# A modulation row made earlier and two gate products ahead of a loop, in a transformer block on one core

## The chip, the core and the metric

The kernel runs on one core of a Trainium2 chip. The metric is the device time of one execution in microseconds (us), median of three runs. Engines: PE is TensorE (matmuls; PEld its weight loads), DVE VectorE, ACT ScalarE, POOL GpSimd, SP the engine that here issues most DMAs.

## The reference, cut to what matters

Two blocks run one after the other on 512 rows of width 1024. The change lies in the first.

```
mod = (cond @ w_ada[l] + b_ada[l]).reshape(b, 6, d)
shift1, scale1, gate1, shift2, scale2, gate2 = [mod[:, i] for i in range(6)]
hn = modulate(rmsnorm(x, norm1_g[l]), shift1, scale1)
proj = hn @ w_in[l]
qa, ka, va, qi, ki, wi, qb, kb, vb, ga, gb = jnp.split(proj, offsets, axis=-1)
ya = dsa_attention(qa, ka, va, qi, ki, wi, rel_bias)      # top-k mask from an index score of qi, ki, wi
yb = stick_breaking_attention(qb, kb, vb)
merged = jax.nn.sigmoid(ga) * (ya @ w_proj_a[l]) + jax.nn.sigmoid(gb) * (yb @ w_proj_b[l])
x = x + gate1[:, None, :] * (merged @ w_out[l])
...
```

`cond` is one vector of 1024 numbers, so each of the six modulation rows is a vector times a 1024 x 1024 piece of `w_ada`. The row of this change is `gate1`, which is first used after `w_out`.

## The kernel before

Everything is laid out with the model's width on the partitions. A matmul of full precision is three fp32r matmuls (lines 189 to 191, high x high, low x high, high x low): weights come by a 512 KB DMA into `raw`, ACT makes the high part `whi` (L183), DVE the low part `wlo` (L184), and 24 matmuls of 128x512 then give 128 output columns for all 512 rows. Such a run of 24 is called a product here. Products, PV sums and the modulation sum go through two PSUM banks `g`, scores and other sums through six banks `a`.

Block 1 goes through these stages (times in the span): norm and first products to 74 us; the **index stage** to about 125 us; **sb**, stick-breaking attention over 8 heads, to 255 us; **DA**, the masked attention over 8 heads, to 372 us; the **w_proj loop** over eight chunks n to 467 us; w_out after it.

In the index stage `vproj` (v of sb) is followed by 24 index units: two matmuls of kih/kil with qi, an ACT relu (L553) and a DVE sum into `iacc` (L555, L557). Then come `z0` and `z1`, the first scores of the sb heads 0 and 1 (L421, L422, L650), and two products for head pair 1 (called q1 and k1 here; they are the first two fills). The bias rows `rs` are made there too (L540 on PE, L541 on DVE).

`heads` runs the heads of sb and DA. Before each half head it calls fills by the table `B1F`: k is a product for a later head's q or k, g a gate product, t a step of the top-k search, v the second vproj, a half of a modulation row (`ada`), r its end (the `row` that `ada` returns). `WPF` is such a table for the w_proj loop.

`ada` loads eight 128x512 pieces of `w_ada`, two to a DMA of 512 KB, into `adaraw` (two buffers), and DVE sums them weighted with `cond` into the accumulator (L305 the first, L307 the other seven: one chain). `row` sums over the partitions on PE with a matrix of ones (L311), adds the bias on DVE (L314; with a gain also L318) and writes 512 numbers to `modrow` in HBM (L319). In DA all chains use one accumulator, `iacc` of the index stage.

Each engine works through its instructions in a fixed order, which a scheduler sets at build time from the program. An engine that waits holds back everything behind it. SP issues the DMAs in order in the same way.

At a DA head's end ACT copies half of the PV sum into `ya` (L455) and DVE adds the other half (L460); only then is that `g` bank free.

Of the kernel before, what the change touches and what calls it, by code (L numbers as in the profile page):

```python
# [11 lines left out]
F32 = mybir.dt.float32  # L12
# [5 lines left out]
AF = mybir.ActivationFunctionType  # L18
# [7 lines left out]
KC = 8  # L26
TB = 4
# [34 lines left out]
WX = 5  # L62
ADV = (5, 5, 5, 6, 7, 8, 8, 8)
B1F = ('kk', 'gt', 'kt', 'kt', 'gt', 't', 'kt', 'kt', 'gt', 't', 'kt', 'kt', 'gt', 'gt', 't', 'v',
       'ka', 'k', 'r', 'gk', 'a', 'k', 'r', 'gk', 'a', 'k', 'r', 'g', 'a', '', 'r', '')
WPF = ('', '', 'a', '', 'ra', 'ra', 'ra', 'r')
ADKB = 3
TG = 4
# [7 lines left out]
class Kern:  # L76
# [214 lines left out]
                nc.tensor.transpose(p[:, ts(t, 128)], src[:, t, ts(k, 128)], self.ident)  # L291
            self.hilo(hi[:, k], lo[:, k], p, None if scale is None else scale[:, k:k + 1])

    def ada(self, pool, acc, cond, col, dst_row, half, gain=None):
        nc, I = self.nc, self.I
        wv = I["w_ada"].rearrange("(k p) n -> p k n", p=128)
        c0 = col * D + half * 512
        for kc in range(0, KC, 2):
            raw = pool.tile([128, 2, 512], F32, tag="adaraw", bufs=2, name=self.nm("adaraw"))
            with self.tc.issue_after(self.loaded):  # L300
                nc.sync.dma_start(raw, wv[:, kc:kc + 2, c0:c0 + 512])
            for j in range(2):
                k = kc + j
                if k == 0:
                    nc.vector.tensor_scalar(acc, raw[:, 0], cond[:, 0:1], None, op0=ALU.mult)  # L305
                else:
                    nc.vector.scalar_tensor_tensor(acc, raw[:, j], cond[:, k:k + 1], acc, op0=ALU.mult, op1=ALU.add)  # L307

        def row():
            p = self.psg()  # L310
            nc.tensor.matmul(p, lhsT=self.onesf, rhs=acc, start=True, stop=True)  # L311
            bro = pool.tile([1, 512], F32, tag="adab", bufs=1, name=self.nm("adab"))
            nc.sync.dma_start(bro, I["b_ada"][0:1, c0:c0 + 512])
            nc.vector.tensor_tensor(acc[0:1], p[0:1], bro, op=ALU.add)  # L314
            if gain is not None:
                bro = pool.tile([1, 512], F32, tag="adab", bufs=1, name=self.nm("adab"))
                nc.sync.dma_start(bro, I[gain][0:1, half * 512:half * 512 + 512])
                nc.vector.scalar_tensor_tensor(acc[0:1], acc[0:1], 1.0, bro, op0=ALU.add, op1=ALU.mult)  # L318
            nc.sync.dma_start(self.modrow[dst_row:dst_row + 1, half * 512:half * 512 + 512], acc[0:1])  # L319
        return row  # L320
# [147 lines left out]
    def block1(self):  # L468
        nc, tc, I = self.nc, self.tc, self.I
        wv = I["w_in"].rearrange("(k p) n -> p k n", p=128)  # L470
        ctx = ExitStack()
        b1 = ctx.enter_context(tc.tile_pool(name="b1", bufs=1))
        hnh, hnl = self.act_pair()
# [12 lines left out]
        def vproj(c0, pool):  # L486
            v = pool.tile([128, TB, 8, 2, 64], F32R, tag="v", name=self.nm("v"))
            for half in range(2):
                outs = [self.psg(), self.psg()]
                for kc in range(0, KC, 4):  # L490
                    hi, lo = self.split_chunk(wv[:, kc:kc + 4, c0 + 256 * half:c0 + 256 * half + 256])
                    for j in range(4):
                        k = kc + j
                        for t in range(TB):
                            self.mm3(outs[t // 2][:, ts(t % 2, 256)], hnh[:, k, ts(t, 128)], hnl[:, k, ts(t, 128)],
                                     hi[:, j], lo[:, j], k == 0 and t % 2 == 0, k == KC - 1, skip=True)
                for i in range(2):
                    self.v_split(v, 2 * i, half, outs[i])
            return v

        with tc.tile_pool(name="p0", bufs=1) as p0:
            cond = self.load_cond(p0)
# [6 lines left out]
        with tc.tile_pool(name="pidx", bufs=1) as pi:  # L509
            pva = pat_ctx.enter_context(tc.tile_pool(name="pva", bufs=1, side="right"))  # L510
            rb = pva.tile([32, 8], F32, name="rb")
            oh = pva.tile([32, 640], F32, name="oh")
            rs = pva.tile([8, 640], F32, name="rs")
            nc.sync.dma_start(rb, I["rel_bias"])
            nc.sync.dma_start(oh, I["bucket"])
            rdr = self.dp.tile([8, 640], F32, name="rdr")
            r128 = self.dp.tile([8, 128, 640], F32, name="r128")
            p = outs[0]
            kih = pi.tile([128, 512], F32R, name="kih")
            kil = pi.tile([128, 512], F32R, name="kil")  # L520
            for q in range(2):
                nc.scalar.activation(kih[64 * q:64 * q + 64], p[0:64], AF.Copy)
            for q in range(2):
                nc.vector.tensor_tensor(kil[64 * q:64 * q + 64], p[0:64], kih[0:64], op=ALU.subtract)
            qi = [self.stack_out(pi, "qi", outs[1], bufs=4)]
            wiT = pi.tile([128, 512], F32, name="wiT")
            nc.scalar.activation(wiT[64:72], p[64:72], AF.Copy, scale=IDX_SCALE)
            pw = self.psg()
            wi = pi.tile([128, TB, 8], F32, name="wi")
            for t in range(TB):  # L530
                nc.tensor.transpose(pw[:, ts(t, 8)], wiT[64:72, ts(t, 128)], self.ident[64:72, 64:72])
            nc.vector.tensor_copy(wi.rearrange("p t h -> p (t h)"), pw[:, 0:32])
            vb = vproj(3144, pvb)
            qi += [self.stack_out(pi, "qi", outs[i], bufs=4) for i in range(2, 5)]
            qk["qb", 0] = self.dup_out(pat, "dup", outs[5], 0.125)
            qk["kb", 0] = self.stack_out(pat, "stk", outs[6])
            acc = {b: b1.tile([128, 128 * (b + 1)], F32, name=f"iacc{b}") for b in range(1, 4)}
            for j, (a0, n) in enumerate(((0, 512), (512, 128))):
                p = self.psg()
                nc.tensor.matmul(p[:8, :n], lhsT=rb, rhs=oh[:, a0:a0 + n], start=True, stop=True)  # L540
                nc.vector.tensor_scalar(rs[:, a0:a0 + n], p[:8, :n], -1.0, None, op0=ALU.mult)  # L541
            nc.sync.dma_start(rdr, rs)
            for h in range(H):
                nc.sync.dma_start(r128[h], rdr[h:h + 1].broadcast_to([128, 640]))
            for pr in range(4):
                for e in range(2):
                    h = 2 * pr + e
                    for b in (3, 2, 1):
                        nk = 128 * (b + 1)
                        s = self.psa()  # L550
                        self.mm2(s[:, :nk], qi[pr][:, e, ts(b, 128)], kih[:, :nk], kil[:, :nk], True, True)
                        rl = pi.tile([128, 512], F32, tag="relu", bufs=3, name=self.nm("relu"))
                        nc.scalar.activation(rl[:, :nk], s[:, :nk], AF.Relu)  # L553
                        if h == 0:
                            nc.vector.tensor_scalar(acc[b], rl[:, :nk], wi[:, b, 0:1], None, op0=ALU.mult)  # L555
                        else:
                            nc.vector.scalar_tensor_tensor(acc[b], rl[:, :nk], wi[:, b, h:h + 1], acc[b],  # L557
                                                           op0=ALU.mult, op1=ALU.add)
# [13 lines left out]
        gates = {}  # L572
# [134 lines left out]
            return pt  # L707

        pad = ctx.enter_context(tc.tile_pool(name="pad", bufs=1))
        adas = [(c, r, hf, g) for c, r, g in ((2, 0, None), (4, 1, "norm2_g"), (3, 2, None), (5, 3, None)) for hf in range(2)]  # L710
        rows = []
        fill["a"] = lambda: rows.append(self.ada(pad, acc[3], cond, *adas.pop(0)))
        fill["r"] = lambda: rows.pop(0)()
# [3 lines left out]
            heads(16, lambda h: da_s(pa, h), lambda st: self.transpose_p(pa, st, 2), va["v"], ya)  # L717
        pat_ctx.close()
        pm = ctx.enter_context(tc.tile_pool(name="pm", bufs=1))
        mh = pm.tile([128, KC, 512], F32R, name="mh")  # L720
        ml = pm.tile([128, KC, 512], F32R, name="ml")
        ys_ctx = ExitStack()
# [22 lines left out]
            for c in WPF[n]:  # L745
                fill[c]()
        xv = I["x"].rearrange("(t p) d -> p t d", p=128)
        for t in range((len(gates) + 1) // 2):
            nc.sync.dma_start(self.x[:, t], xv[:, t])
        ys_ctx.close()  # L750
        prm = ctx.enter_context(tc.tile_pool(name="prm", bufs=1))
# [865 lines left out]
```

## Time and profile before

| what | value |
|---|---|
| median of 3 runs | 2385.33 us (2384.72 to 2385.57) |
| profiled execution | 2384.28 us, its span 2382.4 us |
| PE / DVE / ACT busy | 97% / 73% / 43% of the span |
| chain that ended last | PE 91%, DVE 5% |
| DA stage, 273 to 372 us | PE busy 82.58 of 99 us, mean granted clock 0.90 |

The span is what the trace covers; the profiled execution took 1.9 us more around it. The median of the runs is 1.05 us above the profiled execution. The granted clock is a share of TensorE's full clock: 1.00 is 2.4 GHz, 0.50 is 1.2 GHz.

### The profile page before, as it was taken

The numbers are of one execution on the slowest core, as the hardware profiler recorded it, in microseconds if no ns is written. First come the engines' busy times: TensorE is split into PE (matmuls) and PEld (weight loads), VectorE is DVE, ScalarE is ACT, GpSimd is POOL, SyncE is SP. The second block draws the span as 40 slices with busy tenths as digits, with TensorE's granted clock in tenths as the row PEclk, the third lists the DMA queues.
The fourth block names the chain that finished last, engine by engine and source line by source line (L and its number), as shares of the span: only waits on it lengthen the run. The fifth ranks groups of instructions, "written<-read, shape, count | busy, mean of one in ns | idle before, by whom it ended". The sixth has DMA issues, their size and how long they took to land.

```text
span 2382.4 us, 33726 instructions
## 1 busy us (share of the span) xinstructions
PE 2302.8 (97%) x12405; PEld 2013.1 (85%) x12409; DVE 1744.0 (73%) x3421; ACT 1030.3 (43%) x1642; POOL 326.3 (14%) x286
## 2 busy tenths in 40 slices
PE   7999888999999999999999999999989989999999
PEld 6888766778899999999999988888868878888887
DVE  7689876677998998876888898888886765333321
ACT  3587444243355665553333333333345543322211
POOL 0000000000000323432344432222200000000000
PEclk9999999999999999999999999999989989999999
DMA  9432644652255999989999999999943312333231
GB/s 268 116 98 63 187 141 132 207 165 80 87 179 165 349 357 352 340 337 331 313 334 340 339 376 358 334 338 348 343 136 91 102 36 80 107 97 97 90 116 43
DMA packets 282217, 498.63 MB, mean 209 GB/s; under 512 B 19442, under 2 KB 176754, under 8 KB 280516
## 3 DMA queue, kind: packets, MB, share of 16 engines
q1 hardware_dynamic: 243268, 355.96, 44.8%
q0 software_dynamic: 38784, 140.53, 16.9%
q8 instruction: 97, 1.59, 0.3%
q14 instruction: 68, 0.56, 0.1%
HBM read 444.98 MB, written 47.76 MB: 207 GB/s over the span
## 4 chain that ended last, share of the span: by engine, by line
PE 91%; DVE 5%; ACT 1%; issue 1%; DMA 1%; SPq 0%; DVEq 0%; ACTq 0%
PE a L190 17%; PE a L189 17%; PE a L191 17%; PE g L189 11%; PE g L190 11%; PE g L191 10%; PE g L962 2%; PE a L421 1%; DVE wlo L184 1%; PE g L421 1%; PE g L422 1%; PE a L675 0%; PE a L422 0%; PE a L674 0%; DVE nl L257 0%
## 5 line engine op out<-in xcount | busy, mean ns | idle before, releaser
L183 ACT ACTIVATE whi<-raw 128x1024 fp32r<-128x1024 f32 x425 | 446.5, 1054 | 682.6 <-PE g L190 343.8
L184 DVE TENSOR_TENSOR wlo<-raw,whi 128x1024 fp32r<-128x1024 f32 x425 | 518.2, 1221 | 297.9 <-ACT whi L183 288.1
L189 PE MATMUL g<-nh,whi 128*128 128x512 f32 (+4 forms) x1024 | 384.2, 375 | 10.8 <-DVE ya L460 7.8
L190 PE MATMUL g<-nl,whi 128*128 128x512 f32 (+4 forms) x1024 | 383.3, 374 | 0.0
L191 PE MATMUL g<-nh,wlo 128*128 128x512 f32 (+4 forms) x1024 | 381.4, 372 | 0.0
L190 PE MATMUL a<-nl,whi 128*128 128x384 f32 (+2 forms) x912 | 309.8, 340 | 1.3 <-DVE nl L257 1.2
L189 PE MATMUL a<-nh,whi 128*128 128x384 f32 (+2 forms) x912 | 303.7, 340 | 3.4 <-ACT nh L256 3.3
L191 PE MATMUL a<-nh,wlo 128*128 128x384 f32 (+2 forms) x912 | 305.2, 335 | 0.4 <-DVE wlo L184 0.4
L190 PE MATMUL a<-wlo,ch 128*128 128x512 f32 x768 | 298.6, 389 | 0.0
L191 PE MATMUL a<-whi,cl 128*128 128x512 f32 x768 | 297.9, 389 | 0.0
L189 PE MATMUL a<-whi,ch 128*128 128x512 f32 x768 | 264.0, 389 | 0.0
L1038 POOL DMA_INDIRECT grow<-in_u_dram,eidx x128 | 152.4, 1191 | 764.2 <-DVE o_g L941 433.1
L189 PEld LDWEIGHTS g<-nh,whi 128*128 128x128 f32 (+1 forms) x1024 | 193.0, 188 | 42.3 <-DVE ya L460 8.4
L191 PEld LDWEIGHTS g<-nh,wlo 128*128 128x128 f32 (+1 forms) x1024 | 193.3, 189 | 29.5 <-issue 0.2
L190 PEld LDWEIGHTS g<-nl,whi 128*128 128x128 f32 (+1 forms) x1024 | 193.0, 188 | 29.5
L256 ACT ACTIVATE ch<-cf 128x384 fp32r<-128x384 f32 x128 | 67.1, 525 | 319.3 <-issue 182.9
L1038 POOL DMA_INDIRECT grow<-in_v_dram,eidx x128 | 159.4, 1246 | 318.4 <-DVE gacc L1056 269.7
L189 PEld LDWEIGHTS a<-nh,whi 128*128 128x128 f32 x912 | 173.6, 191 | 6.4 <-ACT nh L256 4.1
L190 PEld LDWEIGHTS a<-nl,whi 128*128 128x128 f32 x912 | 173.4, 190 | 4.6 <-DVE nl L257 2.0
L191 PEld LDWEIGHTS a<-nh,wlo 128*128 128x128 f32 x912 | 174.1, 191 | 2.9 <-DVE wlo L184 0.8
L191 PEld LDWEIGHTS a<-whi,cl 128*128 128x128 f32 x768 | 144.2, 188 | 29.8
L190 PEld LDWEIGHTS a<-wlo,ch 128*128 128x128 f32 x768 | 144.1, 188 | 28.9
(398 smaller groups left out, 3947.6 us busy)
## 6 DMA issues: line engine op xcount, KB each, us to landing
raw<-in_u_t_dram SPq DMA_DIRECT2D x128, 512.0 KB
raw<-in_v_dram SPq DMA_DIRECT2D x128, 512.0 KB
raw<-in_w_in_dram SPq DMA_DIRECT2D x54, 512.0 KB
gdr<-gblk SPq DMA_DIRECT2D x12, 2048.0 KB
vg<-gdr SPq DMA_DIRECT2D x192, 128.0 KB
udr<-ug SPq DMA_DIRECT2D x44, 384.0 KB
vu<-udr SPq DMA_DIRECT2D x44, 384.0 KB
adaraw<-in_w_ada_dram SPq DMA_DIRECT2D x32, 512.0 KB
```

What stands on the lines that cost most here:

```text
L183: nc.scalar.activation(hi, raw, AF.Copy)
L184: self.lastlo = nc.vector.tensor_tensor(lo, raw, hi, op=ALU.subtract).ins
L189: mm(out, lhsT=lh, rhs=rh, start=start, stop=False, skip_group_check=skip)
L190: mm(out, lhsT=lh, rhs=rl, start=False, stop=False, skip_group_check=skip)
L191: mm(out, lhsT=ll, rhs=rh, start=False, stop=stop, skip_group_check=skip)
L256: nc.scalar.activation(hi, src, AF.Copy)
L421: mm(out, lhsT=st, rhs=mh, start=start, stop=False, skip_group_check=skip)
L422: mm(out, lhsT=st, rhs=ml, start=False, stop=stop, skip_group_check=skip)
L962: nc.tensor.matmul(p[:, ts(j, 128)], lhsT=s2[:, c], rhs=rep[k][:, c // 2, :, c % 2], start=(i == 0), stop=(i == 1))
L1038: nc.gpsimd.indirect_dma_start(out=u, out_offset=None, in_=I[src], in_offset=bass.IndirectOffsetOnAxis(ap=eidx[:, i:i + 1], axis=0))
```

## The change

The first modulation row (column 2 of `w_ada`, `gate1`, both halves) leaves the fills of DA. It is made in the index stage right after `vproj`, with its own accumulators `adasum`, and with DMAs of one 128x512 piece (256 KB, eight per half instead of four). The second half of `B1F` is dealt anew: DA keeps the two halves of column 4. `WPF` is as it was. The gate products of chunk n=4 are written ahead of the w_proj loop, and ACT copies them to `gearly`; the loop then finds them in `gates`.

```diff
 B1F = (...
-       'ka', 'k', 'r', 'gk', 'a', 'k', 'r', 'gk', 'a', 'k', 'r', 'g', 'a', '', 'r', '')
+       'k', 'k', '', 'gk', 'a', 'k', '', 'gk', 'r', 'k', 'a', 'g', '', '', 'r', '')
...
-    def ada(self, pool, acc, cond, col, dst_row, half, gain=None):
+    def ada(self, pool, acc, cond, col, dst_row, half, gain=None, ks=2):
...
-        for kc in range(0, KC, 2):
-            raw = pool.tile([128, 2, 512], F32, tag="adaraw", bufs=2, name=self.nm("adaraw"))
+        for kc in range(0, KC, ks):
+            raw = pool.tile([128, ks, 512], F32, tag="adaraw", bufs=2, name=self.nm("adaraw"))
...
             vb = vproj(3144, pvb)
+            for half in range(2):
+                asum = pi.tile([128, 512], F32, tag="adasum", name=self.nm("adasum"))
+                self.ada(pi, asum, cond, 2, 0, half, ks=1)()
...
-        adas = [(c, r, hf, g) for c, r, g in ((2, 0, None), (4, 1, "norm2_g"), (3, 2, None), (5, 3, None)) for hf in range(2)]
+        adas = [(c, r, hf, g) for c, r, g in ((4, 1, "norm2_g"), (3, 2, None), (5, 3, None)) for hf in range(2)]
...
         pm = ctx.enter_context(tc.tile_pool(name="pm", bufs=1))
+        for j in (1, 0):
+            p = self.psg()
+            self.gemmT(self.split_chunk(wv[:, :, (3656, 4680)[j] + 512:(3656, 4680)[j] + 640]), hnh, hnl, p)
+            g = gates[4, j] = pm.tile([128, 512], F32, name=self.nm("gearly"))
+            nc.scalar.activation(g, p, AF.Copy)
...
```

What follows is the order in which the scheduler leaves the instructions, at three places. Line numbers behind L528 are three higher in the changed kernel, and eight higher behind L719; numbers in names differ too.

**DVE at the end of the index stage**, before: the last index sums, then the first step of sb's head 0 (L660).

```order
L557 SCALAR_TENSOR_TENSOR iacc_1000<-relu_1141,wi,iacc_1000 128x256
L184 TENSOR_TENSOR wlo_1399<-raw_1396,whi_1398 128x1024
L260 SCALAR_TENSOR_TENSOR dup_1239<-g_1214,dup_1239 64x512
L557 SCALAR_TENSOR_TENSOR iacc_1002<-relu_1147,wi,iacc_1002 128x512
L557 SCALAR_TENSOR_TENSOR iacc_1001<-relu_1153,wi,iacc_1001 128x384
L557 SCALAR_TENSOR_TENSOR iacc_1000<-relu_1159,wi,iacc_1000 128x256
L260 SCALAR_TENSOR_TENSOR dup_1239<-g_1214,dup_1239 64x512
L660 SCALAR_TENSOR_TENSOR sbt_1178<-a_1166,sbt_1178 128x512
```

The same place in the changed kernel, from the third piece of the second half on (the first, L305, and the second stand seven and four rows earlier, among index sums):

```order
L307 SCALAR_TENSOR_TENSOR adasum_1004<-adaraw_1011,cond,adasum_1004 128x512
L560 SCALAR_TENSOR_TENSOR iacc_1062<-relu_1221,wi,iacc_1062 128x256
L307 SCALAR_TENSOR_TENSOR adasum_1004<-adaraw_1014,cond,adasum_1004 128x512
L307 SCALAR_TENSOR_TENSOR adasum_1004<-adaraw_1017,cond,adasum_1004 128x512
L307 SCALAR_TENSOR_TENSOR adasum_1004<-adaraw_1020,cond,adasum_1004 128x512
L307 SCALAR_TENSOR_TENSOR adasum_1004<-adaraw_1023,cond,adasum_1004 128x512
L307 SCALAR_TENSOR_TENSOR adasum_1004<-adaraw_1026,cond,adasum_1004 128x512
L314 TENSOR_TENSOR adasum_1004<-g_1029,adab_1031 1x512
L544 TENSOR_SCALAR rs<-g_1065 8x512
L544 TENSOR_SCALAR rs<-g_1068 8x128
L663 SCALAR_TENSOR_TENSOR sbt_1240<-a_1228,sbt_1240 128x512
```

The last five sums of the second half now stand in a row, each behind a load of its own, and `rs`, which stood among the index sums, comes after them. The eight sums of the first half stand earlier, during vproj.

**PE behind the scores z1**, changed kernel: the row sum of the second half, the two `rs` matmuls, then q1 (48 matmuls of q1 and k1 follow in a row).

```order
L653 MATMUL a_1346<-strictT,identb 128x128
L311 MATMUL g_1029<-adasum_1004,onesf 128x512
L543 MATMUL g_1065<-oh,rb 8x512
L543 MATMUL g_1068<-oh,rb 8x128
L189 MATMUL g_1276<-nh_174,whi_1272 128x512
L190 MATMUL g_1276<-nl_175,whi_1272 128x512
```

Before, q1 and k1 stood among the index units and between z0 and z1 (g_1252 is k1):

```order
L650 MATMUL a_1168<-strictT,identb 128x128
L191 MATMUL g_1252<-nh_174,wlo_1249 128x512
L189 MATMUL g_1252<-nh_174,whi_1248 128x512
L190 MATMUL g_1252<-nl_175,whi_1248 128x512
L191 MATMUL g_1252<-nh_174,wlo_1249 128x512
```

So both products moved behind L311 of the second half, and behind L543, whose `g` banks they take over.

**PE at the end of DA**, changed kernel, in the last head's PV sum (g_3771). The first gate product is g_3788: 18 of its matmuls stand ahead of the first row below, one is the third row, five come behind the PV sum.

```order
L422 MATMUL g_3771<-ptl_3741,v_2506 128x512
L421 MATMUL g_3771<-pth_3739,v_2506 128x384
L189 MATMUL g_3788<-nh_174,whi_3791 128x512
L422 MATMUL g_3771<-ptl_3742,v_2506 128x384
L421 MATMUL g_3771<-pth_3740,v_2506 128x256
L422 MATMUL g_3771<-ptl_3743,v_2506 128x256
```

Before, the PV matmuls stood there alone and the w_proj loop followed at once. Earlier in DA the changed kernel has no L311 between the first three heads; the scores of heads 6 and 7 stand together behind the PV sum of head 5, where before those of head 6 stood inside the last k product.

## Rows read from the trace of the kernel before

**Rows 1.** Stages: length, busy us by engine, then granted clock, DMA share, GB/s.

```profile
95.00:120.00 25.00, 24.89 (x147) 20.40 (x146) 15.59 (x27) 13.42 (x29) 0.82 (x2) 1.00 0.49 137
120.00:255.00 135.00, 134.10 (x793) 116.41 (x792) 124.20 (x266) 99.68 (x193) 3.27 (x7) 1.00 0.31 80
255.00:273.00 18.00, 14.45 (x66) 11.06 (x66) 16.89 (x43) 10.07 (x25) 0.51 (x1) 0.97 0.90 275
273.00:372.00 99.00, 82.58 (x379) 64.40 (x381) 77.31 (x188) 42.44 (x99) 2.82 (x5) 0.90 0.53 153
372.00:467.00 95.00, 94.78 (x391) 75.14 (x392) 60.23 (x80) 33.41 (x47) 0.00 (x0) 0.97 0.54 162
```

**Rows 2.** DVE's timeline, index stage: start, us, [idle before and its releaser].

```profile
103.52 1.23 DVE L184 TENSOR_TENSOR wlo<-raw,whi 128x1024 fp32r<-128x1024 f32 x1 [0.53 <-ACT whi L183]
107.30 0.67 DVE L541 TENSOR_SCALAR rs<-g 8x512 f32<-8x512 f32 x1
108.77 4.17 DVE L557 SCALAR_TENSOR_TENSOR iacc<-relu,wi,iacc 128x384 f32<-128x384 f32 x8
122.02 1.62 DVE L660 SCALAR_TENSOR_TENSOR sbt<-a,sbt 128x512 f32<-128x512 f32 x3 [2.62 <-ACT sbt L659]
```

**Rows 3.** PE's timeline: q1, k1, the gate product, head 0's suffix sums.

```profile
108.63 0.39 PE L189 MATMUL g<-nh,whi 128*128 128x512 f32 x1
...
114.67 0.40 PE L189 MATMUL g<-nh,whi 128*128 128x512 f32 x1
...
124.18 0.48 PE L189 MATMUL g<-nh,whi 128*128 128x512 f32 x1
...
129.84 0.68 PE L674 MATMUL a<-sph,ntri 128*128 128x512 f32 x3
```

**Rows 4.** SP's and DVE's timelines, DA: loads, row writes, and who waits.

```profile
357.55 0.24 SPq L317 DMA_DIRECT2D adab<-in_norm_g_dram  x1
359.20 0.68 DVE L318 SCALAR_TENSOR_TENSOR iacc<-iacc,adab 1x512 f32<-1x512 f32 x1 [0.63 <-DMA adab<-in_norm_g_dram]
344.35 1.97 SPq L301 DMA_DIRECT2D adaraw<-in_w_ada_dram  x2
348.63 0.75 DVE L307 SCALAR_TENSOR_TENSOR iacc<-adaraw,cond,iacc 128x512 f32<-128x512 f32 x1 [2.74 <-DMA adaraw<-in_w_ada_dram]
276.17 0.25 SPq L319 DMA_DIRECT2D modrow<-iacc  x1
278.98 0.49 DVE L305 TENSOR_SCALAR iacc<-adaraw,cond 128x512 f32<-128x512 f32 x1 [2.64 <-DMA modrow<-iacc]
```

**Rows 5.** PE's waits, 255 to 373 us: total, times, longest.

```profile
PE g L189 <- DVE ya L460: 7.8, 4, 2.9
```

**Rows 6.** Three-microsecond stretches at half clock, columns as in group 1.

```profile
342.00:345.00 3.00, 3.00 (x9) 2.32 (x8) 1.89 (x3) 0.00 (x0) 0.51 (x1) 0.50 0.46 98
375.00:378.00 3.00, 3.00 (x9) 2.32 (x8) 1.53 (x3) 2.97 (x5) 0.00 (x0) 0.52 0.01 3
```

**Rows 7.** PE's timeline, DA: instructions that PE waited for.

```profile
271.76 1.76 PE L311 MATMUL g<-iacc,onesf 128*128 128x512 f32 x2 [2.80 <-DVE iacc L307]
274.58 0.80 PE L421 MATMUL g<-pth,v 128*128 128x512 f32 x1 [1.06 <-DVE dup L257]
...
297.75 0.50 PE L189 MATMUL g<-nh,whi 128*128 128x512 f32 x1 [1.38 <-DVE ya L460]
309.48 0.71 PE L189 MATMUL g<-nh,whi 128*128 128x512 f32 x1 [2.70 <-DVE ya L460]
341.30 0.79 PE L189 MATMUL g<-nh,whi 128*128 128x512 f32 x1 [2.91 <-DVE ya L460]
358.62 1.31 PE L789 MATMUL a<-cst,P 128*128 128x128 f32 x10 [1.53 <-DVE P L779]
368.49 0.50 PE L422 MATMUL g<-ptl,v 128*128 128x512 f32 x1 [0.63 <-DVE ptl L257]
371.96 0.80 PE L189 MATMUL a<-ybh,whi 128*128 128x512 f32 x1 [1.33 <-ACT ybh L256]
```

More of the change, by code (lines that the diff above doesn't have):

```diff
@@ L297, in ada @@
         c0 = col * D + half * 512
-        for kc in range(0, KC, 2):
-            raw = pool.tile([128, 2, 512], F32, tag="adaraw", bufs=2, name=self.nm("adaraw"))
+        for kc in range(0, KC, ks):
+            raw = pool.tile([128, ks, 512], F32, tag="adaraw", bufs=2, name=self.nm("adaraw"))
             with self.tc.issue_after(self.loaded):
-                nc.sync.dma_start(raw, wv[:, kc:kc + 2, c0:c0 + 512])
-            for j in range(2):
+                nc.sync.dma_start(raw, wv[:, kc:kc + ks, c0:c0 + 512])
+            for j in range(ks):
                 k = kc + j
@@ L747, in block1 @@
         xv = I["x"].rearrange("(t p) d -> p t d", p=128)
-        for t in range((len(gates) + 1) // 2):
+        for t in range(TB):
             nc.sync.dma_start(self.x[:, t], xv[:, t])
```

## Prediction

> **What bounds the kernel now.** The table before says that PE is busy 97% of the span and that 91% of the chain that ended last is PE. So the change can win only where PE now stands idle or runs at half clock, and it loses wherever it makes PE idle. I read the stages next [rows 1]: from 95 to 255 us PE has no slack (24.89 of 25 us, then 134.10 of 135, at clock 1.00), although DVE, at 124.20 of 135, is close behind. In 255 to 372 us PE is idle for 18 - 14.45 + 99 - 82.58 = 20.0 us, and the mean clock of 0.90 in the 99 us means up to another 9.9 us of lost PE speed; the w_proj loop is full again but for its first six microseconds, at half clock (0.97 of 95 us, 2.9 us). Together 32.8 us: that is the ceiling of all that the change can give back in DA and at the head of the w_proj loop. The reader is to see that it takes work out of a stage with slack and puts it into one that had none.
>
> **What the change adds in the index stage.** The first half's chain is dealt among DVE's idle time during vproj, ten and more microseconds ahead of what PE needs; SP runs four `raw` loads ahead there. I cost it at nothing; the cover is DVE's slack (15.59 busy of 25 us [rows 1]), and without it its eight sums would cost 8 x 0.7 = 5.6 us.
>
> The second half is the point. In the changed order its chain ends behind the last index sums, PE's L311 stands behind z1 and waits for it, and q1 and k1 stand behind L311. Before, these 48 matmuls filled PE beside the index units, from 108.63 us on [rows 3].
>
> Step by step. DVE still ends `wlo` at about 104.7 [rows 2]. Behind it stand, by the changed order, two v parts, eight index sums and the first half's L314 until L305. Eight index sums took 4.17 us [rows 2], L314 takes as long as the `rs` row, 0.67, the v parts about 0.4 each: L305 starts at about 110. Six index sums of 0.5 us lie between the first four pieces.
>
> The pieces come through two buffers, so each load waits for the sum two pieces earlier. The trace has no load of 256 KB that a sum waits for. Bounds: a row of 2 KB took 357.55 to 359.20, 1.65 us, and a piece of 512 KB 344.35 to 348.63, 4.28 us, with more DMA traffic than here [rows 4]. I take 2.9, about the middle, since half the bytes move in a quieter stage. From L305 on that is 2.3 us for the sums among index sums and three round trips of load and sum, 3 x (2.9 + 0.75 [rows 4]) = 10.95: the chain ends at 110 + 13.25 = 123.3 (bounds 119.5 and 127.4). The Trainium skill (SBUF — State Buffer, "The DMA setup-cost knee") says that a transfer pays about 2 us whatever its size and advises to coalesce, which speaks against splitting the loads into 256 KB; by its fit one such load would take 2.6 us, an estimate, and the chain would end 0.9 us earlier. For 512 KB it gives 3.2 where the row shows 4.28, so the measurement decides and I stay with 2.9.
>
> Then L311 (1.76 us at half clock [rows 7], which PE is at after its idle time), L314 (0.67) and `rs` (0.67), which holds the bank that q1 needs: q1 starts at 123.3 + 3.1 + 0.4 of hops = 126.8. At full clock the 48 matmuls take 48 x 0.234 = 11.2 (24 stand in 129.84 - 124.18 = 5.66 [rows 3]); the start at half clock costs 2.5 more (six microseconds at 0.52 behind the stall at 372 us cost 3 [rows 6]). So head 0's suffix sums start at 140.5, where before they started at 129.84 with the gate product behind them; that product (5.66) now follows. The lag is 140.5 + 5.7 - 129.84 = **16.3 us**, with bounds of 10 (1.65 us a load, no clock loss) and 21 (4.28). Head 0's softplus could be late too: its tiles take the place of the index pool, so ACT waits for the last row's write, 276.17 to 278.98 = 2.8 us [rows 4] behind L314; that gives 129, and with 3.3 us of ACT before DVE's sums (L660 at 122.02 came 3.3 behind ACT's start) it is ready at 137, hidden behind q1 and k1. Nothing of the lag is recovered in sb, which is full of PE work.
>
> **What it gives back in DA.** Two of five chains leave DVE in DA (each 5.7 us), with two L311, two row writes and their waits. PE waited 7.8 us four times for `ya` [rows 5]. One by one:
> - The stall at the start of DA (2.80 + 1.76 + 1.06 us up to 274.58 [rows 7]): the chain that stands there is now that of column 4, and DVE's order up to the `ptl` and `dup` parts that PV waits for is as before. L311 goes, but PV still waits for `dup` until 274.4: 0.2.
> - 297.75: `ya` came as fast as it can there (ACT's copy, DVE's sum, hops: 1.38 [rows 7]). Now the transposes stand behind the product instead of ahead of it, so PE waits the same: 0.
> - 309.48: 2.70 because a chain's first sum stood ahead of `ya`. That chain is gone, a prompt `ya` leaves 1.4: 1.3, and about 1.7 of clock in the six microseconds behind.
> - The third wait, 0.83 long by the sum of the four: no longer behind transposes, 1.1 now: -0.3.
> - 341.30: 2.91. Now ten transposes (1.31 [rows 7]) stand between PV and the product: 2.8, and 2.7 of the clock (0.50 in 342 to 345 [rows 6]).
> - Two L311 less: 0.8.
> - The end. Heads 6 and 7 have their scores together behind everything, so PE waits for head 6's softmax (some 8 us from first score to the last P, DVE's work for two heads): transposes start about where they did, -0.6. The first gate product then fills the last PV sum's waits and the wait for `ybh` (0.63, its like of 0.59, and 1.33 [rows 7], 2.8 with the small one behind), and saves half of the 3 us of half clock at the loop's head: 4.1. The two products themselves are moved, not added; the two copies of ACT lie in its idle time.
>
> The sum is 0.2 + 0 + 3.0 - 0.3 + 5.5 + 0.8 - 0.6 + 4.1 = **12.7 us**. The low end is 5: no clock regained and the end no better. The high end is 22: also the start stall gone by half, and the clock at 1.00 throughout; 32.8 is the ceiling.
>
> **The sum.** 16.3 - 12.7 = +3.6 us against the profiled execution's 2384.28: 2387.9. The median of the runs is 1.05 above that execution, so 2388.9 us for the median, 0.15% above 2385.33.
>
> **The rivals.**
> - *Slower by a clear margin.* The lag comes in full or more, and the waits for `ya` only move: DVE's part in DA is still three chains, and PE then waits for `ptl` or P instead. Place: q1 behind L311. Price: 16 to 21 less 5 to 8, +8 to +14: 2394 to 2399. It decides from a load of 3 us with a gain below 11. For it: DVE is on the way in DA, 77.31 of 99 us [rows 1], and PE's scores of heads 6 and 7 stand late. Against: each wait for `ya` had a chain's sum or a row write ahead of it.
> - *Faster.* The short loads land in 2 us, so the chain ends at 120.6 and the lag is 13.5; and with two chains less, DVE runs so far ahead of PE in DA that the clock stays up, gain 21: -7, 2378. It decides from a gain 5 us above the lag. For it: the 9.9 us of clock loss are all in DA, and each idle stretch avoided saves some. Against: that asks for two thirds of the ceiling, and the first stall stays.
> - *The change hardly does what it says in the index stage*: q1 and k1 are behind L311, but if the loads land as fast as the 2 KB row, the lag is 10, and with the forecast's gain the result is -2.5, 2383. This lies within what can't be told from no change.
> - By the coalescing rule taken strictly, a chain of four 512 KB loads would have beaten this one of eight; it changes only the size of the lag.
>
> **How the numbers follow.** About 0.2% (4.8 us) is what a measurement of this kernel can tell from no change. My forecast with its own spread, 2384 to 2392, has 0.38, nearly all within 0.2%; the fast loads 0.06, the same; the slower rival 0.34; the faster one 0.22. The range leaves out a tenth on either side: 2376 to 2399. Chances: faster 0.21, same 0.43, slower 0.36.
>
> **What would show it.** Right: PE idle for several microseconds after z1, with L311 waiting for DVE's L307, and those waiting for `adaraw`; q1 at about 127 us; the first PV sum of sb, at 140.9 before, near 157; sb still without PE slack; DA's waits for `ya` below 5 us in total; the w_proj loop's head at full clock sooner. Wrong: q1 before 122 us; the start stall of DA gone; new waits of PE for `ptl` or P above 8 us in sum; a clock below 1.00 in sb.

## The result and the profile after

The changed kernel took 2401.09 us (median of 4, 2399.74 to 2402.24) against 2385.43 for the kernel before: ratio 1.0065, 95% interval 1.0052 to 1.0078, so 15.7 us slower. Measured once more it gave 1.0059 (1.0042 to 1.0075). The forecast had the direction, but with +3.6 us, and gave "slower" a chance of 0.36; the time lies 2 us beyond the range.

The stages after, with the columns of [rows 1]; the third to the fifth row lie where sb, DA and the w_proj loop now stand:

```profile
95.00:120.00 25.00, 20.80 (x141) 17.48 (x139) 16.82 (x30) 10.71 (x24) 0.00 (x0) 1.00 0.28 76
120.00:145.00 25.00, 17.95 (x53) 11.80 (x54) 11.85 (x19) 11.80 (x24) 0.94 (x2) 0.66 0.50 148
145.00:270.00 125.00, 124.96 (x733) 108.43 (x732) 116.45 (x251) 87.81 (x169) 3.15 (x7) 1.00 0.30 79
290.00:390.00 100.00, 82.82 (x385) 64.47 (x383) 69.75 (x177) 45.43 (x107) 3.28 (x6) 0.90 0.42 120
390.00:485.00 95.00, 94.88 (x406) 75.39 (x404) 62.91 (x85) 37.68 (x53) 0.00 (x0) 1.00 0.55 164
```

Where PE had no slack it now is busy 38.75 of 50 us, in 25 of them at a mean clock of 0.66. The sb stage behind is as full as before and gives nothing back. In DA PE is idle as long as before (17.2 of 100 us against 16.4 of 99 [rows 1]) although DVE has 7.6 us less to do; only the head of the w_proj loop has its full clock (the mean granted clock of the loop is 1.00 instead of 0.97).

PE's timeline at the stall, changed kernel; q1 starts in the third row:

```profile
126.71 2.05 PE L311 MATMUL g<-adasum,onesf 128*128 128x512 f32 x2 [9.73 <-DVE adasum L307]
128.68 2.30 PE L543 MATMUL g<-oh,rb 32*8 32x512 f32 x4
131.33 0.79 PE L189 MATMUL g<-nh,whi 128*128 128x512 f32 x1 [0.35 <-DVE rs L544]
```

And the chain that it waits for, on DVE (its first sum, then the five sums that waited for their loads), with the first half's row write ahead of it on SP:

```profile
113.16 0.47 DVE L305 TENSOR_SCALAR adasum<-adaraw,cond 128x512 f32<-128x512 f32 x1
...
118.32 0.75 DVE L307 SCALAR_TENSOR_TENSOR adasum<-adaraw,cond,adasum 128x512 f32<-128x512 f32 x1 [0.20 <-DMA adaraw<-in_w_ada_dram]
120.67 0.75 DVE L307 SCALAR_TENSOR_TENSOR adasum<-adaraw,cond,adasum 128x512 f32<-128x512 f32 x1 [1.59 <-DMA adaraw<-in_w_ada_dram]
122.10 0.75 DVE L307 SCALAR_TENSOR_TENSOR adasum<-adaraw,cond,adasum 128x512 f32<-128x512 f32 x1 [0.68 <-DMA adaraw<-in_w_ada_dram]
124.29 0.75 DVE L307 SCALAR_TENSOR_TENSOR adasum<-adaraw,cond,adasum 128x512 f32<-128x512 f32 x1 [1.44 <-DMA adaraw<-in_w_ada_dram]
125.81 0.75 DVE L307 SCALAR_TENSOR_TENSOR adasum<-adaraw,cond,adasum 128x512 f32<-128x512 f32 x1 [0.77 <-DMA adaraw<-in_w_ada_dram]
```

```profile
111.27 0.25 SPq L319 DMA_DIRECT2D modrow<-adasum  x1
```

PE waited 9.7 us for the last sum, then ran the row sum and the two `rs` matmuls at a granted clock of 0.50, and only then q1, which before had started at 108.63 us [rows 3].

### The profile page after: what moved, and what is told of

It reads as the page before. It is cut to its first block, busy times and chain, and to the rows that moved or that the text cites. A ratio compares the mean times of both kernels' runs of the same rounds, so it can differ in the third digit from the quotient of the medians.

```text
span 2397.9 us, 33769 instructions
## 1 busy us (share of the span) xinstructions
PE 2309.7 (96%) x12409; PEld 2017.4 (84%) x12409; DVE 1743.9 (73%) x3421; ACT 1032.4 (43%) x1644; POOL 324.9 (14%) x286
## 4 chain that ended last, share of the span: by engine, by line
PE 79%; DVE 4%; ACT 1%; issue 1%; DMA 0%; DVEq 0%; ACTq 0%
PE a L190 17%; PE a L191 17%; PE a L189 17%; PE g L189 8%; PE g L190 8%; PE g L191 8%; PE g L970 2%; DVE nl L257 0%; PE a L797 0%; PE a L1396 0%; DVE wlo L184 0%; PE g L421 0%; PE g L422 0%; PE g L249 0%; DMA raw<-in_peer_wq_dram 0%
## 5 line engine op out<-in xcount | busy, mean ns | idle before, releaser
L191 PEld LDWEIGHTS a<-whi,cl 128*128 128x128 f32 x768 | 144.2, 188 | 29.9
L190 PEld LDWEIGHTS a<-wlo,ch 128*128 128x128 f32 x768 | 144.2, 188 | 28.7
```

What stands on the lines that cost most here:

```text
L190: mm(out, lhsT=lh, rhs=rl, start=False, stop=False, skip_group_check=skip)
L191: mm(out, lhsT=ll, rhs=rh, start=False, stop=stop, skip_group_check=skip)
```

## Where the time went, stage by stage

I cut each profiled execution at four of PE's instructions: the first and last matmul of the first vproj, the last PV matmul of sb, the first matmul of w_out. The same cuts serve for all experiments; lengths in us, each a difference of two start times in PE's timeline (the last column but two: the rest of the span). "Ratio" is that of the runs to the kernel before.

| kernel | vproj starts | vproj | to the end of sb | DA and w_proj loop | rest | span | ratio |
|---|---|---|---|---|---|---|---|
| before | 74.59 | 27.2 | 151.7 | 213.9 | 1915.0 | 2382.4 | 1 |
| changed | 76.52 | 28.5 | 169.7 | 207.9 | 1915.4 | 2397.9 | 1.0065 |
| changed again | 76.75 | 28.7 | 168.5 | 209.3 | 1915.7 | 2398.9 | 1.0059 |
| gates only | 74.50 | 28.7 | 151.7 | 209.2 | 1914.8 | 2378.9 | 0.9973 |
| row only | 74.64 | 28.6 | 168.3 | 214.2 | 1910.5 | 2396.2 | 1.0064 |
| two accumulators | 74.44 | 29.2 | 153.5 | 207.2 | 1913.8 | 2378.1 | 0.9981 |
| wait alone gone | 76.22 | 29.0 | 153.7 | 209.8 | 1915.7 | 2384.4 | 0.9984 |
| mended, row only | 74.65 | 30.8 | 153.6 | 211.8 | 1913.9 | 2384.8 | 1.0007 |
| four pieces | 74.42 | 29.9 | 161.9 | 210.0 | 1916.3 | 2392.5 | 1.0023 |
| row left out | 74.97 | 26.0 | 151.7 | 213.1 | 1912.0 | 2377.7 | 0.9989 |
| left out, old deal | 76.46 | 27.5 | 151.7 | 211.1 | 1915.0 | 2381.7 | 0.9974 |
| two accumulators, old deal | 75.53 | 29.3 | 153.5 | 211.7 | 1914.1 | 2384.0 | 0.9992 |
| no chain in DA | 74.93 | 27.5 | 151.7 | 205.3 | 1915.5 | 2374.9 | 0.9955 |

The column to the end of sb is the sharpest: 151.7 in all five kernels that leave the index stage alone, 153.5 to 153.7 in the four with a mended row, 168.3 to 169.7 in the three profiles with the change's index stage. The changed kernel's 15.5 us in the span are 1.9 at the start, 1.2 in vproj, 18.0 up to the end of sb, -6.0 in DA and the loop, 0.4 in the rest.

How far one profile can be trusted shows in the columns themselves. Vproj took 28.7 us in the kernel with the gates only, whose program up to there is that of before (27.2), so the changed kernel's 1.2 us in vproj can't be told from chance. Vproj takes 29.2 us on average in the eight profiles with the row beside it (28.5 to 30.8) and 27.4 in the five without (26.0 to 28.7): the row may cost some 2 us there. DA and the loop differ by 1.4 us between the two profiles of the changed kernel.

## The experiments

Theory A, formed on the trace after: both halves of the row use one tile, `adasum`, of one buffer. The first half's sums stay in it until its row write to HBM has read them, so the second half's first sum depends on that write (as in DA before, where a chain's first sum waited 2.64 us for the write of the row ahead of it, [rows 4], at 278.98). The scheduler therefore puts this chain behind the index sums, its row sum behind z1 and q1 and k1 behind the row sum; at its end nothing is left but loads that go round two buffers. Theory B, the rival: sixteen loads and sums in a full stage cost this wherever they stand. For DA: theory D, the gates give all of the gain; theory C, taking the chains out of DA gives the 12 us that were forecast. These letters stand in the expectations.

**The change in two parts.** First the early gate products alone, on the kernel before (the hunk of the diff behind `pm`; beside it the loop that loads `x` has its four steps written out, since they were counted from the gates):

> The kernel before with the two early gate products alone. Theory A (the index stage costs some 19 to 21 us by the order of its instructions, DA gives back some 6): the gates fill the end of DA and keep the w_proj loop's head at full clock, 2 to 4 us faster than before, 2381 to 2383. Rival (the gates bring nothing, all of the gain in DA is the chain's): 2385, within 1 us of before.

2379.9 us against 2385.7, ratio 0.9973 (0.9963 to 0.9982): they gain, and more than the 2 to 4 us expected. DA and the loop take 4.6 us less; the stretches to the end of sb and behind the loop are as before, vproj is 1.5 us longer in this profile. The granted clock of the w_proj loop is 1.00:

```profile
372.00:467.00 95.00, 94.64 (x403) 75.02 (x402) 64.79 (x88) 38.15 (x53) 0.00 (x0) 1.00 0.56 171
```

Then the moved row alone:

```diff
...
-        for j in (1, 0):
-            p = self.psg()
...
-            nc.scalar.activation(g, p, AF.Copy)
```

> The changed kernel without the early gate products. Theory A: 2 to 4 us slower than the changed kernel, 2403 to 2405. Rival (the gates bring nothing): 2401. A rival that the gates cause part of the loss: below 2400.

2399.9 us, 1.0064 (1.0047 to 1.0080). DA and the loop take 214.2, no less than before with two chains more: without the gates the change gains nothing there. The total did not rise above the changed kernel's as I had expected; it lies at the edge of the last rival. In the profile the rest of its span is 4.9 us shorter and its start 1.9 earlier, but the four runs go from 2397.82 to 2404.03 us and the profiled one, 2398.08, is the second fastest; why the rest is shorter there I can't say. That the gates also count beside a moved row shows below: with the row mended the kernel takes 0.9981 of before's time with them and 1.0007 without.

**An accumulator for each half.**

```diff
             for half in range(2):
-                asum = pi.tile([128, 512], F32, tag="adasum", name=self.nm("adasum"))
-                self.ada(pi, asum, cond, 2, 0, half, ks=1)()
+                self.ada(pi, yb[:, 2 + half], cond, 2, 0, half, ks=1)()
```

> The changed kernel with an accumulator of its own for each half of the row (the two last quarters of yb, which is written only later), so that the second half's first sum no longer waits for the first half's row write. Theory A (one accumulator for two halves puts the second chain, its row sum and with them the products q1 and k1 late): the chain ends during or just behind vproj, PE has no stall behind z1, the lag falls from 21 to some 3 to 5 us, and the time to 2383 to 2387. Rival B (16 more loads and sums cost this whatever their place): 2396 to 2401.

2380.86 us, 0.9981 (0.9971 to 0.9990): 20 us faster than the changed kernel with the same loads, sums and matmuls, and a little faster than theory A had it. That refutes B. What it leaves open is whether it helped that `yb` is outside the index stage's pool, on whose release head 0's softplus waits. In the changed kernel ACT stood idle for the row write:

```profile
130.77 1.36 ACT L660 ACTIVATE sbt<-a 128x512 f32<-128x512 f32 x3 [14.42 <-DMA modrow<-adasum]
```

So the next kernel moves the first half alone, and the second half's row write still holds the pool:

```diff
-                asum = pi.tile([128, 512], F32, tag="adasum", name=self.nm("adasum"))
+                asum = pi.tile([128, 512], F32, tag="adasum", name=self.nm("adasum")) if half else yb[:, 3]
```

> The changed kernel with only the first half's accumulator moved to yb; the second half keeps adasum in the index stage's pool, so head 0's softplus still waits for its row write. Theory A (the one accumulator was the cause): as with two in yb, 2379 to 2384. Rival (what helped there was that the softplus no longer waited for a row write behind the pool): 2390 or more.

2382.04 us, 0.9984 (0.9975 to 0.9994), and 153.7 us to the end of sb, as with two in `yb` (153.5). PE's timeline there: both row sums follow each other 15.6 us before the time at which the changed kernel has its second.

```profile
109.62 1.10 PE L311 MATMUL g<-yb,onesf 128*128 128x512 f32 x2 [0.29 <-DVE v L257]
111.09 1.02 PE L311 MATMUL g<-adasum,onesf 128*128 128x512 f32 x2
```

So the shared accumulator is the cause: 16.0 of the 18.0 us go with it (some 14.6 to 15 by the other two profiles of this index stage), and some 2 stay, about what the two row sums take on PE (1.10 + 1.02). The write of the second row is issued at 116.93 us here, and the softplus starts at 119.17 without waiting for it. So the wait on the pool went with the late chain; what it would cost with PE's stall gone was not tried.

**How the price of the stall is made up.** The second half's sum over four of its eight pieces:

```diff
-        for kc in range(0, KC, ks):
+        for kc in range(0, kn, ks):
...
-                self.ada(pi, asum, cond, 2, 0, half, ks=1)()
+                self.ada(pi, asum, cond, 2, 0, half, ks=1, kn=KC if half == 0 else 4)()
```

> The changed kernel with four of the eight pieces in the second half's sum (the other four are left out of the row). Theory A (q1 and k1 wait for the end of this chain, whose last pieces go round two buffers at 3.7 us for two): the chain ends 7.4 us earlier, and so does all behind it: 2393 to 2395 against 2401. Rival (PE's start behind z1 is set by something else, such as the row's write and the pool that ACT waits for): 2399 to 2401.

2391.37 us, 1.0023 (1.0013 to 1.0033). The stretch to the end of sb falls by 7.8 us from the changed kernel's 169.7 (by 6.5 from its second profile), as theory A has it. The total falls by 9.7 between the medians, to 1.6 below A's range, and by 5.4 between the two profiled spans. PE there waits 2.43 us for the chain instead of 9.73:

```profile
118.77 2.05 PE L311 MATMUL g<-adasum,onesf 128*128 128x512 f32 x2 [2.43 <-DVE adasum L307]
```

**DA without the row.** With the row left out altogether and all else as changed:

```diff
-            for half in range(2):
-                asum = pi.tile([128, 512], F32, tag="adasum", name=self.nm("adasum"))
-                self.ada(pi, asum, cond, 2, 0, half, ks=1)()
+            nc.sync.dma_start(self.modrow[0:1, :], I["b_ada"][0:1, 2 * D:3 * D])
```

> The changed kernel with the first modulation row left out: its bias alone is copied to the row, no load or sum of w_ada for it, the new deal and the early gates kept. So it shows what DA gains when the index stage pays nothing. Theory A: 5 to 7 us faster than before, 2378 to 2380. Rival C (DA gains the 12 us that were forecast, and the index stage loses more than the trace's stages say): 2373.

2381.34 us, 0.9989 (0.9980 to 0.9999): outside both forecasts, and no faster than the gates alone, which make the row in DA. It is no clean measure, since the scheduler dealt the order anew and put head 6's scores where nothing covered the copy of its q; PE's timeline has one wait that no other kernel has:

```profile
350.30 0.77 PE L421 MATMUL a<-dup,stk 128*128 128x512 f32 x1 [8.99 <-DMA dup<-dup]
```

So I left the row out with the fills at their places of before (B1F's 'a' and 'r' of the first row blank, the others unmoved):

> As the kernel with the row left out (its bias alone), but the other fills of DA at their places of before. Theory D (the gates give all of DA's gain; without the chains PE's waits only move to other parts of the softmax): as the gates alone, 2377 to 2382. Rival C (the waits at 309 and 341 us go with the chain that stood ahead of them): 2371 to 2375.

2381.2 us, 0.9974 (0.9964 to 0.9985), the same as the gates alone, with the row's work simply gone. PE's waits in DA and at the loop's head sum to 21.6 us there (257 to 382 us) and to 19.8 with the gates alone (256 to 379 us). Theory D. The same deal with two accumulators in the index stage:

> The kernel with two accumulators, with the other fills of DA at their places of before. Theory A and D: the index stage pays some 4 us, the gates give 5: 2380 to 2384, no better than the gates alone. Rival C: 2374 to 2378.

2384.89 us, 0.9992 (0.9982 to 1.0001), a little above what D expected. And no modulation chain among DA's fills at all ("it" is the kernel with the row left out, which this one changes further):

> As before it, and rows 0 and 1 both of the bias alone: no modulation chain among DA's fills (one of the later rows may be placed at its end by the scheduler). Theory D: at least 10 us of PE's waits in DA stay, since they are those of the softmax itself; 2372 to 2380. Rival C (DVE's chains make the waits): PE waits below 6 us in DA, 2362 to 2368.

2376.37 us, 0.9955 (0.9938 to 0.9971). PE's waits in that DA, 252 to 375 us (total, times, longest):

```profile
PE g L189 <- DVE ya L460: 7.0, 4, 4.5
PE g L422 <- DVE ptl L257: 5.1, 6, 2.5
PE a L421 <- DVE st L782: 3.0, 2, 1.7
PE g L189 <- DVE v L257: 1.4, 1, 1.4
PE a L796 <- DVE P L786: 0.9, 1, 0.9
PE g L421 <- ACT pth L256: 0.7, 1, 0.7
PE g L189 <- DVE dup L257: 0.7, 1, 0.7
```

They add to 18.8 us, against 19.8 with the gates alone, with 7.0 for `ya` where the kernel before has 7.8 [rows 5]. Taking all four chains out of DA's fills hardly shortens PE's waits. Against the gates alone DA and the loop take 3.9 us less, about what four row sums cost PE (1.02 each at full clock in DA). This decides between C and D.

**What the moved row is worth once mended**, without the gates:

> The kernel with two accumulators without the early gate products: the moved row alone, mended. Theory D (taking the chains out of DA gives nothing, the index stage pays some 3.5 us): 2386 to 2390. Rival C (the move is worth something once its stall is mended): 2379 to 2384.

2387.46 us, 1.0007 (0.9997 to 1.0016): no gain. The stretch to the end of sb pays 1.9 us and vproj up to 3.6 (it varies, as said above), DA and the loop give 2.1 back. The last run repeats the changed kernel beside the two kernels that mend it:

> The changed kernel itself once more, beside the two others on one chip: 2399 to 2403 by every theory; and whether its first 60 us, 1.9 us later in its profile than before's with the same instructions in the same order, are later again (then they belong to the change) or not (then to the single execution).

2400.15 us. Its vproj starts 2.2 us late again. But so it does in the kernel with the wait alone gone and in one that has no row in the index stage at all (76.46), while four pieces starts at 74.42; in the four late ones (76.2 to 76.8) the profile's first 25 us show a clock of 1.00, in the others (74.4 to 75.5) 0.88 to 0.95. I can't tie it to the change; what sets it stays open.

## Why the prediction went wrong, point by point

- *The lag of 16.3 us.* The mechanism was right: q1 and k1 behind the row sum, the row sum behind the chain, the chain at the pace of its loads, nothing recovered in sb. At the end of sb the lag was 21.2; its upper bound, by its own terms 20.4 and not 21, was passed. The chain was forecast to end at 123.3; it ended near 126.5, which is 123.3 plus the 3.1 us by which vproj ended late. Every second of the sums that waited came 3.6 to 3.8 us after the last but one, so a load took 2.9 to 3.0 where I had taken 2.9: that term held. (By the fit of the Trainium skill, SBUF — State Buffer, "The DMA setup-cost knee", it would be 2.6, an estimate; the trace shows more here too.) Three terms were short, together by 4.4 of the 4.9 us: the start, 1.9, and vproj, 1.2, neither of which can be put down to the change, and the way from the chain's end to q1, 4.8 instead of 3.5, because the first `rs` matmul at half clock (2.30 for the two) stands there too.
- *What I had not seen in the lag.* I priced the chain's place without asking what put it there. The data were at hand: in the order that I read, the chain's first sum stands behind the first half's L314, and both work on the one tile. Had I read the dependency on the one `adasum` buffer, the rival to weigh would have been a kernel with two.
- *The gain of 12.7 us* is the step that failed. It came to 6.0 (4.6 in the second profile). The end of DA with the gates was forecast at 4.1 (its parts, 2.8 and half of 3, make 4.3) and gave 4.6 by itself. That sum held in part by luck: with the gates alone PE's waits fall by 1.1 in all (20.9 to 19.8), not by 2.8, and the loop's clock (0.97 to 1.00 over 95 us) gives back about 2.9, not half of 3. The rest, 8.6 us, came to nothing (214.2 us for DA and the loop with the moved row alone, 213.9 before). Nearly all of it, 8.5, was the waits for `ya` at 309 and 341 us with the clock behind them: the first was to go with the chain ahead of it, the second to be filled by transposes. In the changed kernel PE waits 4.9 us for `ya` instead of 7.8, as I had expected ("below 5 us in total"), but the same time turned up elsewhere. PE's waits in the changed kernel, 276 to 396 us:

```profile
PE g L189 <- DVE ya L460: 4.9, 3, 2.4
PE g L422 <- DVE ptl L257: 4.4, 5, 2.7
PE a L421 <- DVE st L783: 3.2, 2, 2.2
PE a L797 <- DVE P L787: 2.5, 3, 1.0
PE g L189 <- DVE stk L260: 2.3, 1, 2.3
```

  And in the kernel before, 255 to 373 us, beside the 7.8 for `ya` [rows 5]:

```profile
PE g L422 <- DVE ptl L257: 3.1, 5, 1.3
PE g L311 <- DVE iacc L307: 2.8, 1, 2.8
PE a L789 <- DVE P L779: 1.5, 1, 1.5
PE a L421 <- DVE st L775: 1.2, 1, 1.2
PE g L421 <- DVE dup L257: 1.1, 1, 1.1
```

  With the small ones (1.4 for v and 0.2 for `pth` after; 1.7 for v, 1.5 for the loop's `ybh` and `ybl` and 0.2 for `pth` before) the waits are 18.9 us after and 20.9 before. The waits for `ya`, `iacc` and `dup` fell by 6.8 us, those for `ptl`, `st`, P and `stk` rose by 6.6. The rows named a chain's sum ahead of `ya`; but the kernel without the row and the one without any chain show waits of about the same sum (21.6 and 18.8) under other names. I read this as PE waiting in DA for one head's softmax after another, so that it reaches the next wait sooner when one goes.
- *The rivals.* "Slower by a clear margin" was what happened in both its parts: the lag in full, and DA's waits only moved. I gave it 0.34, and took 5 to 8 us for a gain that was 6; the time is 2 us above its 2394 to 2399. The faster rival asked for DVE ahead of PE in DA to keep the clock up: the stage's mean clock is 0.90 as before. The rival with loads as fast as the 2 KB row fell with the 2.9 to 3.0 us; the one with four loads of 512 KB was not run.
- *The sum.* 16.3 became 21.5 (with the rest of the span), 12.7 became 6.0: +15.5 in the span, +15.7 in the runs. Both bounds together, 21 - 5 = 16 above, lay beyond the range's end; it should have held that.
- *What would show it.* Right: L311 waiting for DVE, sb without slack, q1 late (131.3 instead of about 127), the first PV sum of sb late (161.9 instead of 157), `ya` below 5, the loop's head at full clock. Of the signs against it, new waits for `ptl` or P above 8 us in sum did not come (6.9 in all, 4.6 before), but with `st` and `stk` these waits are 12.4 where they were 5.8.

The early gates alone, at 0.9973, beat the kernel before and the changed one; none of the kernels that compute all of the reference and move the row was faster than they are.

## What to carry to other kernels

A scratch tile that ends in a DMA write to HBM stays in use until that write is done (the 2.64 us wait of [rows 4]); where the next use came from the same one buffer, the scheduler put it late, and everything that stands in order behind it went with it. So ask of a chain that stands oddly late which tile it waits for, before pricing its place. And a wait "for" an instruction that stood behind other work on a busy engine need not go away with that work, if a chain of dependent steps runs just behind it (here 18.8 us of waits with no chain among the fills, 19.8 with four): leave the work out altogether in a trial, and look whether the sum of the waits falls.

## What was not expected of the hardware

Behind the 9.7 us stall the granted clock was 0.50 from 126.7 to 131.3 us: the two matmuls of the row sum took 2.05 us there and the four of `rs` 2.30, against 1.02 for the two of a row sum at full clock in DA. With q1's first fourteen matmuls at half clock too the stall costs more than its idle time. In the ten profiles whose program is the same in order to 60 us, the first vproj starts between 74.4 and 76.8 us.
